# Splits of the fillers' weights ahead of the substitution, four tiles of them for three, and the loop for crowded experts inside group 10: one hybrid block on one core

## The chip, the cores and the metric

The kernel runs on one core of a Trainium2 chip. The time is device microseconds of one execution; the kernel before took 1620.69 us, the median of three runs from 1618.52 to 1622.68.

## The reference, cut to what matters

One residual block on 512 frames of width 1024, with three branches that are gated, projected and summed, and then a mixture of experts:

```
h  = rmsnorm(x); p = h @ w_in                      # conv, RWKV-7 and attention inputs
A  = B * conv3(C * u)                              # short gated convolution
Bw = rwkv7(r, k, v, decay, a)                      # delta-rule state, 8 heads of 64, 512 steps
M  = attention(q, rmsnorm(mem))                    # 4 heads, 256 memory rows
z  = sum_i sigmoid(h @ W_g_i + b_g_i) * (branch_i @ W_p_i)
x  = x + z @ w_o
h2 = rmsnorm(x)
g  = argmax(softmax(h2 @ w_router_group))          # one group of 8 experts
e  = top2(softmax(h2 @ w_router_expert in group g))
x  = x + sum_e weight_e * (silu(h2 @ gate_e) * (h2 @ up_e)) @ down_e
out = rmsnorm(x)
```

All inputs, weights and the output are fp32. There are 64 experts of 1024 x 512, 6 MB each.

## The kernel before, in words

**Dense products.** A weight tile of 128 x 512 arrives in fp32 (`wsrc`) and is split in `split_w` (L77 to L86): ScalarE (ACT) copies it to `wh` (L82, a rounded form), and then `wl` = `wsrc` - `wh` (L85) is made on GpSimd (POOL), or for every third tile on VectorE (DVE). `mm3` (L92) makes of it 12 matmuls of 128 x 512, three for each of four steps of k: `wh` by the high part of the activations, `wh` by the low part, `wl` by the high part. The tiles with the tag "f" have three buffers, those with "r" two.

**Fillers.** RWKV-7 is done in two passes (`rwkv_pass`), each on four heads in chunks of 64. Each pass has one long stretch on DVE: a triangular system is solved by substitution, 31 steps of a product (`tmp`, L405) and a sum (`Xb`, L407), after four transposes into `Ub` (L397) and before two transposes out of `Xb` (L412, L413). The first result of these is `X`, for which the next matmuls of TensorE (PE) wait (L425). Meanwhile PE runs dense products that do not hang on the pass: gates (`gate`, L538), projections (`proj`, whose DVE work is L543 and L545) and the convolution branch (`cu`, `cv`, `ych`, `ycl`, L557 to L569). They are written ahead of the pass or beside it, use the tag "f" and the PSUM name "pf", and are called fillers here. A scheduler puts the instructions of each engine in order when the program is built, by priority: an instruction written earlier has priority over a later one, and what is written under `tc.high_priority(n)` is moved up by n places.

**From the passes to the experts.** After the second pass come the fillers that were not needed as cover, then eight rounds of the last projection (L670 to L675) with a chain `G`, `z`, `zh`, `zl` on DVE and ACT (L543, L545, L673, L674), then eight rounds of `w_o` (L688 to L720), each with a slice `xs` of the input, its square `sq` and a sum `sqs` of the squares on POOL (L708), then the router.

**Experts.** The 64 experts are done in 20 groups of three (g = 0 to 19) and a last group of four. A group has nine loads of 2 MB from SyncE's (SP's) queue, all issued at L640: three `gate` matrices into ring `wa`, three `up` into `wb`, three `down` into `wc`. `select` gathers the group's tokens by matmuls with a one-hot matrix (`oe`, `oT`, `pt`, L820 to L841), `into` multiplies by gate or up (`pc`, `pco`), `hidden` makes the hidden activations `ht`, and `mlp` multiplies by down (`pr`) and adds to `acc` (L883). `mlp` of group g also runs `select` and the gate product of group g + 1, passed as the generator `nxt`. `ahead(3)` issues the next three loads where a ring's last readers have been written; `owed` counts such issues that are to be left out.

An expert with more than 32 tokens is finished by `overflow` (L966 on), a loop whose count is only known on the chip; a pass of it loads one whole expert into ring `wc`. With these inputs it makes no pass. It stands at the start of group 10: `mlp(9)` runs without a next group, the loop follows, then the remaining loads of group 10 are issued, then `begin(10)` selects and multiplies by gate. The SP rows at L969 are the loop's compare and branch.

Of the kernel before, what the change touches and what calls it, by code (L numbers as in the profile page):

```python
# [7 lines left out]
F32 = mybir.dt.float32  # L8
F32R = mybir.dt.float32r
I32 = mybir.dt.int32  # L10
U32 = mybir.dt.uint32
AF = mybir.ActivationFunctionType
OP = mybir.AluOpType
# [4 lines left out]
T, D, MEM = 512, 1024, 256  # L18
NT, ND = T // 128, D // 128
# [23 lines left out]
GE, NG = 3, 20  # L43
# [7 lines left out]
def block_kernel(ctx, tc, I, out):  # L51
    nc = tc.nc
# [11 lines left out]
    def f(ap):  # L64
        return ap.bitcast(F32)
# [5 lines left out]
    wpool = {"f": pro.enter_context(tc.tile_pool(name="wf", bufs=2))}  # L71
# [4 lines left out]

    def split_w(src, shape, tag="f"):  # L77

        n = 3 if tag == "f" else 2
        wh = wpool[tag].tile([128] + shape, F32R, name="wh", bufs=n)  # L80
        wl = wpool[tag].tile([128] + shape, F32R, name="wl", bufs=n)
        nc.scalar.activation(wh, src, AF.Copy)  # L82
        cnt[0] += 1
        eng = nc.gpsimd if cnt[0] % 3 else nc.vector
        eng.tensor_tensor(wl, src, f(wh), op=OP.subtract)  # L85
        return wh, wl  # L86

    def mm3(ps, wh, wl, xh, xl, nk, first=True, last=True, skip=False):
# [31 lines left out]
    yk = keep2.enter_context(tc.tile_pool(name="yk", bufs=1))  # L120
    yr = [yk.tile([128, T], F32, name=f"yr{k}") for k in range(4)]
# [51 lines left out]
    with ExitStack() as attn:  # L173
# [3 lines left out]
        with tc.tile_pool(name="xin", bufs=1) as xin, tc.tile_pool(name="mem", bufs=1) as mp:  # L177
# [3 lines left out]
            xs = xin.tile([128, NT, D], F32, name="xs")  # L181
# [16 lines left out]
            for k in range(ND):  # L198
                wv = wpool["r"].tile([128, 512], F32, name="wv", tag="wsrc", bufs=4)
                nc.sync.dma_start(wv, I["w_v"][k * 128:(k + 1) * 128])  # L200
                wh, wl = split_w(wv, [512], "r")
# [82 lines left out]
    for nm, t in (("ln_x_w", lnw), ("ln_x_b", lnb)):  # L284
        v = I[nm].rearrange("o (q e j c) -> o q e j c", q=2, e=2, j=2)
# [285 lines left out]
    for m in range(ND):  # L571
        g = fil.tile([128, T], F32, name="g", bufs=2)
# [32 lines left out]
    sl, so = (late.tile([128, 2, NT], F32, name=n) for n in ("sl", "so"))  # L605
    vals = late.tile([128, 2, NT, 6], BF, name="vals")
    ring = {n: ctx.enter_context(tc.tile_pool(name="ring" + n, bufs=1, side="right")) for n in "ab"}
# [37 lines left out]
    def ahead(n):  # L645

        for _ in range(n):
            if owed[0]:
                owed[0] -= 1
            else:  # L650
                next(loads, None)
# [31 lines left out]


    tp = pro.enter_context(tc.tile_pool(name="tp", bufs=2))
    sqs = tp.tile([128, T], F32, name="sqs", bufs=1)
    lg = psum.tile([128, NT, 80], F32, name="lg", tag="pc")
    for m in range(ND):  # L688
        xs = yk.tile([128, NT, 128], F32, name="xs", tag=f"yr{(m + 3) % 4}")
        nc.sync.dma_start(xs, I["x"].rearrange("(t p) d -> p t d", p=128)[:, :, m * 128:m * 128 + 128])  # L690
        ps = acc_r("pf")
        for t in range(NT):
            nc.tensor.matmul(ps[:, t * 128:(t + 1) * 128], xs[:, t], ident, is_transpose=True,
                             start=t == 0, stop=False, skip_group_check=True)
        dense(ps, I["w_o"][m], lambda k: zh[k], lambda k: zl[k], first=False)
        ahead(2)
        x2t = tp.tile([128, T], F32, name="x2t")
        nc.scalar.activation(x2t, ps, AF.Copy)
        sq = sqs if m == 0 else tp.tile([128, T], F32, name="sq")
        nc.scalar.activation(sq, ps, AF.Square)  # L700
        if m == 1:
            sr = tp.tile([128, 1], F32, name="sr", bufs=1)
            nc.scalar.activation(sr, sq[:, 0:1], AF.Sqrt)
        for t in range(NT):
            nc.tensor.matmul(lg[:, t, 0:72], x2t[:, t * 128:(t + 1) * 128], wr[:, m], start=m == 0 and t == 0,
                             stop=False, skip_group_check=True)
        if 0 < m < ND - 1:
            nc.gpsimd.tensor_tensor(sqs, sqs, sq, op=OP.add)  # L708
        if m >= ND - 2:
            s = sqs if m == ND - 2 else sq  # L710
            for t in range(NT):
                nc.tensor.matmul(lg[:, t, 72:73], s[:, t * 128:(t + 1) * 128], one, start=False,
                                 stop=m == ND - 1 and t == NT - 1, skip_group_check=True)
        pt = acc_r("pr")
        for t in range(NT):
            nc.tensor.transpose(pt[:, t * 128:(t + 1) * 128], x2t[:, t * 128:(t + 1) * 128], ident)
        nc.scalar.activation(acc[:, :, m * 128:m * 128 + 128], pt.rearrange("p (t c) -> p t c", t=NT), AF.Copy)
        if m < ND - 1:
            keep_x2(m, pt)
# [131 lines left out]
                ahead(GE)  # L851
            yield ps

    def hidden(sel, pg, wu, rows, nxt):

        *_, pu = into("pco", sel, wu, rows)
        next(nxt, None)
        hid = mo.tile([128, 512], F32, name="hid")
        nc.scalar.activation(hid, pg, AF.Silu, scale=sel[2])
        nc.vector.scalar_tensor_tensor(hid, pu, sel[2], hid, op0=OP.mult, op1=OP.mult)  # L860
        ht = mo.tile([128, 4, 128], F32, name="ht")
        ps = psum.tile([128, 4, 128], F32, name="pc")
        for k in range(4):
            pe.transpose(ps[:, k], hid.rearrange("s (p k) -> s k p", k=4)[:, k], ident)
        nc.scalar.activation(ht, ps, AF.Copy)
        next(nxt, None)
        return ht
# [14 lines left out]
                pe.matmul(pm[:, u], oh[:, (t + u) * 128:(t + u + 1) * 128], y, start=i == 0, stop=i == 1)  # L882
        nc.vector.tensor_tensor(acc[:, t:t + n, cs], acc[:, t:t + n, cs], pm, op=OP.add)  # L883

    def mlp(sel, pg, wu, wd, rows, nxt=iter(()), wg=None):

        next(nxt, None)
        ht = hidden(sel, pg, wu, rows, nxt)
        py = [psum.tile([128, 512], F32, name="pr", bufs=2) for n in range(2)]
        for k in range(4):  # L890
            for n in range(2):
                for a, r in enumerate(rows):
                    pe.matmul(py[n][r], ht[:, k, r], wd(a, k * 1024 + n * 512, 512),
                              start=k == 0, stop=k == 3, skip_group_check=True)
        if len(rows) > 1:
            ahead(GE)
        nsel = next(nxt, None)
        gate = into("pc", nsel, wg, rows) if nsel else iter(())
        for n in range(2):
            ys = weighted(py[n], sel)  # L900
            pg = next(gate, None)
            for t in range(NT):
                combine(t, slice(n * 512, n * 512 + 512), ys, sel[3])
                if t % 2:
                    pg = next(gate, None)
        for pg in gate:
            pass
        return nsel, pg
# [57 lines left out]
    def overflow():  # L966

        n_over = nc.values_load(nov[0:1, NO:NO + 1], min_val=0, max_val=NO)
        with tc.For_i(0, n_over, 1):  # L969
            e = nc.values_load(nov[0:1, 0:1], engines=[mybir.EngineType.SP], min_val=0, max_val=63)  # L970
            t = ring["c"].tile([128, 3, 4096], F32, name="wc")
            ws = []
            for i, n in enumerate(("gate", "up", "down")):
                nc.sync.dma_start(t[:, i], whole(I["w_exp_" + n][bass.ds(e, 1)].rearrange("o k c -> (o k) c")))
                ws.append(lambda a, o, c, i=i: t[:, i, o:o + c])
            mlp(*begin(so, 0.0, ws[0], ALL), ws[1], ws[2], ALL)
            V.tensor_scalar(so, so, 128.0, None, op0=OP.subtract)
            sh = mo.tile([128, NO], I32, name="sh")
            V.tensor_copy(sh[:, 0:NO - 1], nov[:, 1:NO])
            V.tensor_copy(nov[:, 0:NO - 1], sh[:, 0:NO - 1])  # L980

    def begin(at, base, wg, rows):
        *_, sel = select(at, base)
        *_, pg = into("pc", sel, wg, rows)
        return sel, pg

    def weights(g):

        if g < NG:
            s = nc.values_load(whose[0:1, g:g + 1], engines=[mybir.EngineType.PE], min_val=0, max_val=GE - 1)  # L990

        def of(n):
            def w(a, o, c):
                if g < NG and a == GE:
                    return B[g, n][:, bass.ds(s, 1), o:o + c].rearrange("p s c -> p (s c)")
                return W[g, n][a][:, o:o + c]
            return w

        return [of(n) for n in ("gate", "up", "down")]

    ALL, EACH = (slice(0, 128),), tuple(slice(a * CAP, a * CAP + CAP) for a in (1, 2, 3, 0))
    sel = select(sl, 0.0, V)
# [53 lines left out]
    V.tensor_scalar(nof[:, 0:NO], nof[:, 0:NO], 63.0, None, op0=OP.min)  # L1056
    V.tensor_copy(nof[:, NO:NO + 1], bs[:, 64:65])
    V.tensor_copy(nov, nof)
    V = nc.vector
    for g in range(NG + 1):  # L1060
        if g == NG // 2:
            overflow()
            ahead(GE)
            w = weights(g)
            now = begin(sl, 128.0 * g, w[0], EACH)
        if g == NG:
            for _ in loads:
                pass
            finish(*now, *w[1:], EACH)
        elif g + 1 == NG // 2:  # L1070
            owed[0] = GE
            mlp(*now, *w[1:], EACH)
        else:
            v = weights(g + 1)
            now = mlp(*now, *w[1:], EACH, select(sl, 128.0 * (g + 1)), v[0])
            w = v


# [91 lines left out]
```

## Time and profile before

| | |
|---|---|
| runs before, median (lowest to highest) | 1620.69 us (1618.52 to 1622.68) |
| the profiled execution's own time | 1627.8 us |
| its span, and instructions | 1626.0 us, 23087 |
| mean granted clock of PE | 0.935 |
| busy: PE, DVE, ACT, POOL | 1445.8, 615.0, 362.4, 236.2 us |
| read from HBM, mean rate | 452.47 MB, 280 GB/s |

The span divides in two. To about 696 us it is the three branches, the merge and the router; from there the experts. In the first part PE does most of the work under a chain that passes to DVE in each pass; in the second the loads are back to back. In the rows below "a <- b" after a wait is what ended it, `out<-in` are the program's tiles, and xN counts instructions. PEclk is the granted clock of PE as a share of full speed.

### The profile page before, as it was taken

The page shows a single profiled execution, that of the slowest core. Times are in us where ns is not written, and L with a number is a line of the kernel's source. Part 1 is how long each engine was busy: PE and PEld are TensorE (multiplying, and loading weights), DVE is VectorE, ACT ScalarE, POOL GpSimd, SP SyncE. Part 2 cuts the span into 40 slices and gives each one's busy share as a digit, 9 for nine tenths or more (in the row PEclk, how much of TensorE's full clock was granted, in tenths as well). Part 3 has the DMA queues.
Part 4 walks back from the last instruction along what each step waited for, and adds up shares of the span by engine and source line. Part 5 has one row for each costly group of instructions (what it writes and reads, how often), then busy time and mean ns, then how long its engine had stood idle before and what let it go on. Part 6 is the DMA issues. An engine that isn't in the chain of part 4 may idle for free.

```text
span 1626.0 us, 23087 instructions
## 1 busy us (share of the span) xinstructions
PE 1445.8 (89%) x9526; PEld 900.1 (55%) x9526; DVE 615.0 (38%) x1137; ACT 362.4 (22%) x688; POOL 236.2 (15%) x200
## 2 busy tenths in 40 slices
PE   7999978999988999699888899878988888998865
PEld 5777757776766778544444445434444444444423
DVE  5342799257692460532222221213222222222212
ACT  6443432534423444110000000000000000000003
POOL 3224342244431333000000000000000000000001
PEclk9999999899996999799999999998999999999977
DMA  7321212021111195389999999998999999999994
GB/s 247 99 83 49 68 52 79 33 72 59 39 58 40 59 321 189 155 362 430 429 430 429 431 430 431 430 430 376 430 429 430 430 430 431 430 430 430 430 416 190
DMA packets 67721, 456.09 MB, mean 280 GB/s; under 512 B 8984, under 2 KB 15008, under 8 KB 44320
## 3 DMA queue, kind: packets, MB, share of 16 engines
q1 hardware_dynamic: 66016, 453.53, 68.2%
q8 instruction: 78, 1.28, 0.3%
q10 hardware_dynamic: 1600, 1.06, 0.2%
q14 instruction: 27, 0.22, 0.0%
HBM read 452.47 MB, written 2.10 MB: 280 GB/s over the span
## 4 chain that ended last, share of the span: by engine, by line
PE 50%; DMA 32%; DVE 13%; issue 2%; SPq 1%; ACT 1%; POOL 0%; DVEq 0%; ACTq 0%; POOLq 0%
DMA wa<-in_w_exp_gate_dram 27%; PE pc L735 11%; PE pf L92 11%; PE pr L92 7%; PE pf L735 6%; PE pt L735 3%; PE pco L735 2%; DMA wb<-in_w_exp_gate_dram 2%; PE pr L735 2%; DMA wb<-in_w_exp_up_dram 2%; DVE tmp L405 2%; DVE Xb L407 1%; DVE Ub L397 1%; DMA wa<-in_w_exp_down_dram 1%; DVE wl L85 1%
## 5 line engine op out<-in xcount | busy, mean ns | idle before, releaser
L735 PE MATMUL pc<-wa,xgt 128*32 128x512 f32 (+1 forms) x1328 | 218.1, 635 | 73.4 <-DMA wa<-in_w_exp_gate_dram 73.4
L883 DVE TENSOR_TENSOR acc<-acc,pf 128x512 f32<-128x512 f32 x168 | 109.4, 684 | 209.2 <-PE pf L735 209.0
L85 POOL TENSOR_TENSOR wl<-wsrc,wh 128x512 fp32r<-128x512 f32 x101 | 139.8, 1388 | 292.5 <-ACT wh L82 246.6
L735 PE MATMUL pt<-oT,x 128*128 128x128 f32 x1344 | 163.7, 282 | 12.0 <-DVE eg L735 7.1
L735 PEld LDWEIGHTS pt<-oT,x 128*128 128x128 f32 x1344 | 158.4, 197 | 28.7 <-issue 23.2
L735 PE MATMUL pco<-wb,xgt 128*32 128x512 f32 (+1 forms) x1312 | 165.4, 600 | 7.3 <-issue 4.2
L735 PE MATMUL pr<-wc,ht 128*32 128x512 f32 (+2 forms) x1312 | 156.3, 595 | 4.6 <-DMA wc<-in_w_exp_down_dram 3.8
L951 POOL TENSOR_TENSOR acc<-acc,x 128x1024 f32<-128x1024 f32 x3 | 7.1, 2357 | 946.9 <-ACT junk L948 946.9
L735 PEld LDWEIGHTS pc<-wa,xgt 128*32 128x32 f32 x1328 | 40.7, 112 | 180.2 <-DMA wa<-in_w_exp_gate_dram 103.2
L82 ACT ACTIVATE wh<-wsrc 128x512 fp32r<-128x512 f32 x152 | 95.7, 630 | 174.7 <-PE pf L92 86.9
L92 PE MATMUL pf<-hh,wl 128*128 128x512 f32 x288 | 122.8, 426 | 9.9 <-DVE wl L85 9.7
L92 PE MATMUL pf<-hh,wh 128*128 128x512 f32 x288 | 121.0, 420 | 5.8 <-DVE Xb L407 4.1
L735 PEld LDWEIGHTS pco<-wb,xgt 128*32 128x32 f32 x1312 | 76.9, 111 | 86.0 <-issue 65.6
L873 ACT ACTIVATE yh<-pr,wr 128x512 fp32r<-128x512 f32 (+1 forms) x44 | 29.4, 668 | 413.9 <-PE pf L735 224.1
L92 PE MATMUL pf<-hl,wh 128*128 128x512 f32 x288 | 119.7, 416 | 0.0
L735 PEld LDWEIGHTS pr<-wc,ht 128*32 128x32 f32 x1312 | 50.4, 111 | 91.6 <-issue 79.6
L860 DVE SCALAR_TENSOR_TENSOR hid<-pco,wr,hid 128x512 f32<-128x512 f32 x21 | 15.8, 751 | 215.2 <-PE pco L735 215.2
L735 PEld LDWEIGHTS pf<-yh,oh 128*128 128x128 f32 x176 | 37.9, 215 | 91.1 <-issue 46.8
L735 PE MATMUL pf<-yh,oh 128*128 128x512 f32 (+1 forms) x176 | 85.9, 490 | 1.3 <-ACT yh L873 1.0
L874 DVE SCALAR_TENSOR_TENSOR yl<-pr,wr,yh 128x512 fp32r<-128x512 f32 (+1 forms) x44 | 31.8, 723 | 140.5 <-ACT yh L873 140.5
L829 DVE TENSOR_TENSOR xgt<-pt,gft 128x512 f32<-128x512 f32 x40 | 27.7, 692 | 129.0 <-PE pt L735 129.0
L735 PE MATMUL pf<-yl,oh 128*128 128x512 f32 (+1 forms) x176 | 75.3, 430 | 1.2 <-DVE yl L874 1.2
(400 smaller groups left out, 2098.9 us busy)
## 6 DMA issues: line engine op xcount, KB each, us to landing
wc<-in_w_exp_down_dram SPq DMA_DIRECT2D x60, 2048.0 KB, 30.3
wa<-in_w_exp_gate_dram SPq DMA_DIRECT2D x60, 2048.0 KB, 24.6
wb<-in_w_exp_up_dram SPq DMA_DIRECT2D x59, 2048.0 KB, 31.2
wsrc<-in_w_in_dram SPq DMA_DIRECT2D x56, 256.0 KB, 2.6
wsrc<-in_w_gate_dram SPq DMA_DIRECT2D x48, 256.0 KB, 2.6
wsrc<-in_w_branch_dram SPq DMA_DIRECT2D x24, 256.0 KB, 2.7
wa<-in_w_exp_gate_dram SPq DMA_DIRECT2D x12, 512.0 KB, 6.0
wb<-in_w_exp_up_dram SPq DMA_DIRECT2D x12, 512.0 KB, 6.8
```

The costliest lines, as they stand in the source:

```text
L82: nc.scalar.activation(wh, src, AF.Copy)
L85: eng.tensor_tensor(wl, src, f(wh), op=OP.subtract)
L92: nc.tensor.matmul(ps, w(k), x(k), start=first and k == 0 and i == 0, stop=last and k == nk - 1 and i == 2, skip_group_check=skip)
L397: nc.vector.transpose(Ub[rows].rearrange("b t s -> b (t s)"), src.unsqueeze(2).to_broadcast([32, 32, 32 // NB, NB]))
L405: nc.vector.tensor_tensor(tv, Ub[:, s + 1:, s:s + 1].to_broadcast([128, n, s + 1]), Xb[:, s:s + 1, 0:s + 1].to_broadcast([128, n, s + 1]), ...
L407: nc.vector.tensor_tensor(Xb[:, s + 1:, 0:s + 1], Xb[:, s + 1:, 0:s + 1], tv, op=OP.add)
L735: return lambda *a, **k: tc.keep_in_program_order(getattr(self.eng, name)(*a, **k))
L829: V.tensor_tensor(xgt[:, k4:k4 + 4], ps, last(gft[:, k4:k4 + 4], 128), op=OP.mult)
L860: nc.vector.scalar_tensor_tensor(hid, pu, sel[2], hid, op0=OP.mult, op1=OP.mult)
L873: nc.scalar.activation(yh, py, AF.Copy, scale=sel[1])
L874: nc.vector.scalar_tensor_tensor(yl, py, sel[1], f(yh), op0=OP.mult, op1=OP.subtract)
L883: nc.vector.tensor_tensor(acc[:, t:t + n, cs], acc[:, t:t + n, cs], pm, op=OP.add)
```

## The change: three edits

1. `split_w` has four buffers instead of three for the tag "f", and the two instructions of such a split stand under `tc.high_priority(4000)`.
2. To make room, `sqs` takes an existing tile (`yr2`), `xs` goes round three tiles instead of four, and `sq` has one buffer instead of two.
3. `mlp(9)` is now an ordinary one that selects group 10 and multiplies by its gate. In group 10 `hidden` runs first, into a pool of its own; then the loop, which now uses ring `wb`; then three issues that were owed and `mlp(10)` with the finished `ht`, which selects group 11.

```diff
     def split_w(src, shape, tag="f"):
 
-        n = 3 if tag == "f" else 2
-        wh = wpool[tag].tile([128] + shape, F32R, name="wh", bufs=n)
-        wl = wpool[tag].tile([128] + shape, F32R, name="wl", bufs=n)
-        nc.scalar.activation(wh, src, AF.Copy)
+        n = 4 if tag == "f" else 2
         cnt[0] += 1
         eng = nc.gpsimd if cnt[0] % 3 else nc.vector
-        eng.tensor_tensor(wl, src, f(wh), op=OP.subtract)
+        with tc.high_priority(4000) if tag == "f" else ExitStack():
+            wh = wpool[tag].tile([128] + shape, F32R, name="wh", bufs=n)
+            wl = wpool[tag].tile([128] + shape, F32R, name="wl", bufs=n)
+            nc.scalar.activation(wh, src, AF.Copy)
+            eng.tensor_tensor(wl, src, f(wh), op=OP.subtract)
         return wh, wl
...
-    sqs = tp.tile([128, T], F32, name="sqs", bufs=1)
+    sqs = yk.tile([128, T], F32, name="sqs", tag="yr2")
...
-        xs = yk.tile([128, NT, 128], F32, name="xs", tag=f"yr{(m + 3) % 4}")
+        xs = yk.tile([128, NT, 128], F32, name="xs", tag=f"yr{(3, 0, 1)[m % 3]}")
...
-        sq = sqs if m == 0 else tp.tile([128, T], F32, name="sq")
+        sq = sqs if m == 0 else tp.tile([128, T], F32, name="sq", bufs=1)
...
-    def mlp(sel, pg, wu, wd, rows, nxt=iter(()), wg=None):
+    def mlp(sel, pg, wu, wd, rows, nxt=iter(()), wg=None, ht=None):
...
-        ht = hidden(sel, pg, wu, rows, nxt)
+        ht = ht or hidden(sel, pg, wu, rows, nxt)
...
-        nsel = next(nxt, None)
+        nsel = None
+        for nsel in nxt:
+            pass
...
-            t = ring["c"].tile([128, 3, 4096], F32, name="wc")
+            t = ring["b"].tile([128, 3, 4096], F32, name="wb")
...
     for g in range(NG + 1):
-        if g == NG // 2:
-            overflow()
-            ahead(GE)
-            w = weights(g)
-            now = begin(sl, 128.0 * g, w[0], EACH)
         if g == NG:
...
-        elif g + 1 == NG // 2:
+            break
+        ht = None
+        if g == NG // 2:
+
             owed[0] = GE
-            mlp(*now, *w[1:], EACH)
-        else:
-            v = weights(g + 1)
-            now = mlp(*now, *w[1:], EACH, select(sl, 128.0 * (g + 1)), v[0])
-            w = v
+            ht = hidden(*now, w[1], EACH, iter(()), late2)
+            overflow()
+            ahead(GE)
+            w = weights(g)
+        v = weights(g + 1)
+        now = mlp(*now, *w[1:], EACH, select(sl, 128.0 * (g + 1)), v[0], ht)
+        w = v
```

The end of the second pass's substitution on DVE, before (L412 and L413 are the transposes out of `Xb`, L543 the product of a projection's filler, L85 the split):

```order
L407 TENSOR_TENSOR Xb<-Xb,tmp 128x31
L412 STREAM_TRANSPOSE X_2676<-Xb 128x1024
L413 STREAM_TRANSPOSE Ub<-Xb 128x1024
L543 SCALAR_TENSOR_TENSOR g<-g,pf 128x512
L85 TENSOR_TENSOR wl<-wsrc,wh 128x512
L469 COPY RH<-pc 128x128
```

and in the change, where every line number after L80 is higher by one:

```order
L408 TENSOR_TENSOR Xb<-Xb,tmp 128x31
L544 SCALAR_TENSOR_TENSOR g<-g,pf 128x512
L86 TENSOR_TENSOR wl<-wsrc,wh 128x512
L413 STREAM_TRANSPOSE X_2676<-Xb 128x1024
L414 STREAM_TRANSPOSE Ub<-Xb 128x1024
L470 COPY RH<-pc 128x128
```

A split and a product of the fillers that stood behind the transposes now stand ahead of the first of them. Along the rest of the substitution each split stands 4 to 13 rows earlier. Counted to the first transpose out of `Xb`, DVE has as many splits as before in both passes (17, and 12 from the first pass's result on); new ahead of it are one `ycl` (L75) in the first pass and this `g` in the second. In the normalisation of the first pass's result (L497 to L510) two splits now stand that stood around it, in the second pass's two instead of one, and in the chain `G`, `z`, `zh`, `zl` three instead of two.

The loads on SP around the loop, before (`nov` holds the loop's count; L974 are the loop's own loads):

```order
L640 DMA wc<-in_w_exp_down_dram 128x4096 x3
L640 DMA wa<-in_w_exp_gate_dram 128x4096 x3
L640 DMA wb<-in_w_exp_up_dram 128x4096
L968 TENSOR_LOAD nov
L969 COMPARE_AND_BRANCH
...
L969 UNCONDITIONAL_BRANCH
L640 DMA wb<-in_w_exp_up_dram 128x4096 x2
L968 ISA x2
L640 DMA wc<-in_w_exp_down_dram 128x4096 x3
```

and in the change:

```order
L641 DMA wa<-in_w_exp_gate_dram 128x4096 x3
L641 DMA wb<-in_w_exp_up_dram 128x4096 x3
L641 DMA wc<-in_w_exp_down_dram 128x4096 x3
L971 TENSOR_LOAD nov
L972 COMPARE_AND_BRANCH
...
L972 UNCONDITIONAL_BRANCH
L641 DMA wa<-in_w_exp_gate_dram 128x4096 x3
L971 ISA x2
L641 DMA wb<-in_w_exp_up_dram 128x4096 x3
```

Before, the loop stands behind the fourth load of group 10; now it stands behind all nine. In both, nothing is issued between the loop's first compare and its last branch but the loop's own loads, and SP's branch into the loop waits for all loads issued so far and for the other four engines.

Of the fillers' matmuls on PE, counted in order, these stand ahead of a place in the program:

| place on PE | before | after |
|---|---|---|
| first matmul of the first pass's low-rank products | 145 | 152 |
| first `AR` by `BK` product of the first pass | 210 | 210 |
| second block's first product of `sk` by `cst` | 228 | 231 |
| last `AR` by `BK` product of the first pass | 279 | 277 |
| `X`, first pass | 444 | 448 |
| first pass's result transposed | 578 | 589 |
| second pass's first product of `sk` by `cst` | 601 | 610 |
| first `AR` by `BK` product of the second pass | 650 | 654 |
| last `AR` by `BK` product of the second pass | 723 | 726 |
| `X`, second pass | 869 | 876 |
| second pass's result transposed | 1002 | 1012 |
| first `w_o` round's router product | 1179 | 1179 |

## Rows read from the trace of the kernel before

**Rows 1.** The page: busy time by engine, and its chain by engine.

```profile
PE 1445.8 (89%) x9526; PEld 900.1 (55%) x9526; DVE 615.0 (38%) x1137; ACT 362.4 (22%) x688; POOL 236.2 (15%) x200
...
PE 50%; DMA 32%; DVE 13%; issue 2%; SPq 1%; ACT 1%; POOL 0%; DVEq 0%; ACTq 0%; POOLq 0%
```

**Rows 2.** Chain that ended last, start of the experts: start us, length us, what.

```profile
688.90 7.00 PE pc L735 x64
...
773.34 28.69 DMA wa<-in_w_exp_gate_dram
```

**Rows 3.** The same chain around the loop.

```profile
1089.26 26.84 DMA wb<-in_w_exp_up_dram
...
1116.41 0.04 DVEq L969
```

**Rows 4.** Windows around the loop: length, busy us of PE, PEld, DVE, ACT, POOL, PEclk, DMA, GB/s.

```profile
1100.00:1110.00 10.00, 8.66 (x57) 3.30 (x49) 3.83 (x6) 1.38 (x2) 0.00 (x0) 1.00 1.01 431
1110.00:1120.00 10.00, 4.93 (x13) 3.12 (x14) 4.98 (x9) 0.00 (x0) 0.00 (x0) 0.68 0.55 208
1120.00:1130.00 10.00, 10.00 (x80) 9.29 (x83) 2.07 (x5) 0.60 (x1) 0.00 (x0) 0.80 1.01 429
```

**Rows 5.** Windows at the end of the first pass's substitution.

```profile
270.00:280.00 10.00, 5.61 (x19) 3.92 (x18) 9.64 (x24) 1.20 (x2) 2.62 (x2) 0.87 0.22 78
280.00:290.00 10.00, 9.29 (x100) 7.34 (x100) 4.30 (x4) 6.24 (x8) 0.00 (x0) 0.79 0.08 28
290.00:300.00 10.00, 10.00 (x83) 7.37 (x80) 0.44 (x2) 4.30 (x9) 3.26 (x6) 0.66 0.09 28
```

**Rows 6.** Windows at the end of the second pass's substitution.

```profile
480.00:490.00 10.00, 5.04 (x20) 3.22 (x18) 9.52 (x18) 1.84 (x3) 4.12 (x3) 0.95 0.09 25
490.00:500.00 10.00, 5.89 (x47) 4.77 (x48) 5.48 (x11) 3.80 (x4) 1.28 (x1) 0.54 0.16 56
500.00:510.00 10.00, 10.00 (x113) 8.05 (x110) 0.69 (x1) 4.70 (x9) 1.01 (x3) 0.64 0.09 28
510.00:520.00 10.00, 10.00 (x55) 7.18 (x53) 1.44 (x5) 3.54 (x9) 3.05 (x6) 0.51 0.07 27
```

**Rows 7.** Timeline of DVE in the first pass's substitution: start us, us, what.

```profile
264.48 0.42 DVE L407 TENSOR_TENSOR Xb<-Xb,tmp 128x252 f32<-128x252 f32 x1
264.93 1.39 DVE L405 TENSOR_TENSOR tmp<-Ub,Xb 128x247 f32<-128x247 f32 x1
...
276.46 0.68 DVE L85 TENSOR_TENSOR wl<-wsrc,wh 128x512 fp32r<-128x512 f32 x1
```

**Rows 8.** Timeline of POOL, both passes: in brackets the idle time before, and its releaser.

```profile
264.52 1.53 POOL L85 TENSOR_TENSOR wl<-wsrc,wh 128x512 fp32r<-128x512 f32 x1 [1.27 <-ACT wh L82]
...
451.18 1.30 POOL L85 TENSOR_TENSOR wl<-wsrc,wh 128x512 fp32r<-128x512 f32 x1 [6.78 <-ACT wh L82]
```

**Rows 9.** Chain that ended last, the transposes into Ub of the second pass.

```profile
449.87 2.04 DVE Ub L397
451.92 2.02 DVE Ub L397
```

**Rows 10.** PE's waits from 0 to 696 us: total us, times, longest us.

```profile
PE pf L92 <- DVE wl L85: 9.7, 3, 3.6
...
PE pr L425 <- DVE X L412: 5.8, 2, 5.1
```

**Rows 11.** Chain that ended last, from the second pass to w_o.

```profile
567.18 15.07 PE pf L92 x66
582.27 0.70 DVE G L543
...
607.26 0.70 DVE zl L674
608.00 0.73 PE pf L92 x2
...
611.31 4.81 PE pf L92 x21
```

More of the change, by code (lines that the diff above doesn't have):

```diff
@@ L852, in into, with hidden @@
             yield ps
-    def hidden(sel, pg, wu, rows, nxt):
+    def hidden(sel, pg, wu, rows, nxt, pool=mo):
         *_, pu = into("pco", sel, wu, rows)
@@ L860, in hidden @@
         nc.vector.scalar_tensor_tensor(hid, pu, sel[2], hid, op0=OP.mult, op1=OP.mult)
-        ht = mo.tile([128, 4, 128], F32, name="ht")
+        ht = pool.tile([128, 4, 128], F32, name="ht")
         ps = psum.tile([128, 4, 128], F32, name="pc")
@@ L1058, in block_kernel @@
     V.tensor_copy(nov, nof)
+    late2 = ctx.enter_context(tc.tile_pool(name="late2", bufs=1))
     V = nc.vector
     for g in range(NG + 1):
-        if g == NG // 2:
-            overflow()
-            ahead(GE)
-            w = weights(g)
-            now = begin(sl, 128.0 * g, w[0], EACH)
         if g == NG:
```

## The prediction

> **What bounds the kernel now.** I read the page first, then the chain of waits, then windows of time where the chain changes hands. On the page [rows 1] PE is busy 1445.8 of 1626.0 us, but the chain that ended last is only half PE; 32% is loads and 13% DVE. So the kernel has stages with different limits.
>
> From the first gate product at 688.90 [rows 2] the experts run behind loads: every group puts one wait for `wa` of some 28 us into the chain (28.69 us at 773.34 is the first). What a full stretch moves is 431 GB/s [rows 4], so a 2 MB load takes 2.097 / 0.431 = 4.87 us, and a group of nine takes 43.8. Here PE is not the bound. Two things follow: whatever moves the start at 688.90 moves the end by as much, and every microsecond in which loads stand still counts in full.
>
> The loads stand still once. Around the loop the window from 1110 to 1120 moves 208 GB/s where its neighbours move 431 and 429 [rows 4]: (430 - 208) / 430 x 10 = 5.2 us lost. The chain says why [rows 3]: a load issued at 1089.26 is waited for to 1116.1, the loop's branch ends at 1116.45, and loads are issued again only then.
>
> Ahead of the experts, the ends of the two substitutions decide. DVE is busy 9.64 of 10 us from 270 to 280 [rows 5] and 9.52 from 480 to 490 [rows 6], PE 5.61 and 5.04: DVE is the bound, PE the cover. When `X` comes, PE goes on, at a lower clock: 0.79 and 0.66 in the two windows after the first pass's `X`, and 0.54, 0.64 and 0.51 from 490 to 520 in the second. A level of 1.2 GHz is half of 2.4, so a window of mean 0.54 has lost 4.6 us of its ten: 2.1 + 3.4 = 5.5 us after the first `X`, 4.6 + 3.6 + 4.9 = 13.1 after the second. PE waits for DVE's splits 9.7 us in three pieces and for `X` 5.8 in two [rows 10].
>
> **The change, part by part.**
>
> *Fillers.* A split feeds 12 matmuls, and 21 of them take 4.81 us [rows 11], 0.229 each. The table in the section on the change shows where they went; I sort its stretches by who leads there. Where PE leads: +7 ahead of the first pass, +3 between its two blocks of low-rank products, +7 between the first `X` and the transposed result, -2 and -1 on the way into the second pass, +3 after the second `X`, -10 in the rest. That is +7 matmuls, +1.6 us. The same 7 leave stretches that DVE leads (-7, -5 and -5 in the pass's preparation, +6 and +4 under the substitutions), where they cost or save PE nothing: PE has idle time there, 4.4 of ten us in the first window [rows 5].
>
> *DVE's chains.* A split on DVE takes 0.68 us [rows 7], and `ycl` and `g` are of the same shape. To `X` there are no more splits than before, so the earlier places cost nothing, but `ycl` in the first pass and `g` in the second now stand ahead of `X`: 2 x 0.68 = +1.4. Two splits in the first normalisation: between 0 and 2 x 0.68, since fillers cover part of it; I take half, +0.7. In the second, 66 matmuls of fillers (15.07 us) stand behind it [rows 11] and hide the split. The chain from `G` at 582.27 to `zl` at 607.96 [rows 11] has no cover left, since PE starts its next matmul on `zl` at 608.00: one split more, +0.7 (a zero is the other end, as each round also waits for PE). Together +2.8, bounds +1.4 to +3.5.
>
> *POOL.* Two thirds of the splits are POOL's, and they are dear to DVE. A `tmp` that stands beside a POOL split takes 1.39 us, its neighbour 0.42 [rows 7, 8]: about 1.0 us each. The transposes into `Ub` took 2.04 and 2.02 with a POOL split (451.18) beside the second [rows 8, 9], so there it is free. A fourth tile lets one more split start ahead in each window: 0 to 2 x 1.0 us, and below zero if the extra one falls under the transposes. Since +6 and +4 matmuls are less than one split, I take 0 and keep +2 as the end. The Trainium skill ("SBUF — State Buffer", section "SBUF: two separate sides") calls this an exclusive lock: of DVE with two SBUF inputs and GpSimd, whichever comes second stands still until the first has finished. By that, priority for POOL's splits speaks against the change, and the sum would have the whole +2; the rows of `tmp` and of the transposes (one input) agree with it.
>
> *Tiles given up.* `xs` and `sq` are needed once in a round of `w_o`, which has at least its 21 matmuls of 4.81 us on PE [rows 11]; the POOL sum that reads `sq` is of a split's shape, 1.30 us [rows 8]. So one buffer is enough while PE leads: cost 0. If that cover goes, six rounds could each wait for a sum, 6 x 1.3 = 8 us; I give that no weight, as 3.5 us would have to go first.
>
> *The loop.* Before, 1 + 3 loads are in flight at the entry and the fourth one runs alone at the end. After, the order on SP puts all nine ahead, and the branch still waits for the last; behind it six loads are free to go at once. So loads run dry all the same, behind `down` of group 10 instead of the first `up`. `down` lands six loads behind gate, 29 us. `up` lands after 14.6, its product takes as long as gate's (7.00 us for 64 matmuls [rows 2]), and the rest of `hidden` is a few matmuls; so PE should be done by 22 to 25 and not come later than the loads. The gap is between none (-5.2) and doubled (+5.2, if the end of `hidden` came late). Three loads end together instead of one alone, so the old gap may get a little shorter; I choose a fifth of it, -1.0.
>
> *Sum:* +1.6 + 2.8 + 0 + 0 - 1.0 = +3.4 us. The profiled execution took 1627.8 us by its own clock (span 1626.0), which is 7.1 above the median of the runs; it would come to 1631.2. Taken to the median, 1620.7 + 3.4 = **1624.1 us**. About 0.3%, or 4.9 us, is what a measurement of this kernel can tell from no change: from 1615.8 to 1625.6 it counts as the same.
>
> **The rivals.**
>
> *A. The waits for the splits were on the path.* If the splits' new places give PE work without a break, the 9.7 us [rows 10] leave the path, not only PE's idle time: 1624.1 - 9.7 = 1614.4; and if the clock in the second pass then loses only what the first loses, another 13.1 - 5.5 = 7.6 less, 1606.8. For it: these are PE's longest waits for a filler. Against: DVE is busy 95% or more under them, and X hangs on DVE. Chance 0.25.
>
> *B. The pause moves against `X` (slower).* In the first pass the last split on DVE, at 276.46 [rows 7], comes late, and PE then has fillers until shortly before `X`; in the second PE has none left in its last 5 us and waits up to 5.1 us for `X` [rows 10]. The clock loses 5.5 us after the first and 13.1 after the second [rows 5, 6]. If every split is early, the first pass too uses its fillers up and pauses in one piece at the end, and then restarts slowly as the second does now: +7.6, 1631.7, and up to 1633.7 with POOL's 2 us. It decides if PE's pause directly ahead of the first `X` becomes like that ahead of the second. For it: the order on DVE has all splits earlier. Against: the number of fillers ahead of `X` grows too. Chance 0.25. The Trainium skill ("TensorE: Matmul & The Clock Gate", section "HAM oscillation — how this bites in real kernels") tells of kernels whose every burst restarts at half rate after a wait. [...]
>
> *C. The gap at the loop goes.* If the loads behind the loop start without a break, -5.2 instead of -1.0: 1619.9. Against: the order on SP still holds every issue back behind the branch. Chance 0.12.
>
> *D. Nothing moves.* The order is only an order: a split still waits for its load, ACT's copy and a free tile, and POOL idles 1.27 to 6.78 us ahead of one, each time until ACT's `wh` [rows 8]. If tiles, not priority, are what lacks, all stays: 1620.7. Chance 0.06.
>
> **How the numbers follow.** My forecast has 0.32, of which 0.08 lies above 1625.6 (DVE's and POOL's terms at their upper ends). Faster: A, 0.25, and 0.02 for C together with a part of A, 0.27. The same: 0.24 + 0.10 + 0.06 + 0.01 of B, 0.41. Slower: 0.24 + 0.08 = 0.32. Both signs hold much, so the forecast's own range is 1618.5 to 1627.8: the low bounds give +1.6 + 1.4 - 5.2 = -2.2, the high ones +1.6 + 3.5 + 2 = +7.1, without a doubled gap. For eight times in ten I take in B wholly, and with it the doubled gap (1633.0), and of A its first value with some room: 1610 to 1634.
>
> **What the changed profile would show.** Right: PE's waits for DVE's `wl` below 4 us; DVE still 95% busy until `X` in both passes; the first gate product some 4 us later; one gap in the loads of about 4 us, some 24 us later than before. For A the pass ends earlier by 5 us or more and the windows behind `X` have a higher clock; for B the windows behind the first `X` fall to about 0.55. The prediction is wrong if the time from the start to the first gate product moves by more than 5 us, or if no window around the loop falls under 400 GB/s.

## The result, and the profile after

The changed kernel takes 1638.1 us, the median of five runs from 1636.71 to 1645.26; the kernel before takes 1620.01 beside it. The ratio is 1.0115, with a 95% interval from 1.0098 to 1.0131: 18 us slower. The forecast was 1624.1 with no measurable change, and the range ended at 1634.

The page after, with busy time and the chain by engine, in the order of [rows 1]:

```profile
PE 1449.8 (89%) x9526; PEld 898.3 (55%) x9526; DVE 622.5 (38%) x1137; ACT 362.0 (22%) x688; POOL 229.0 (14%) x200
...
PE 48%; DMA 32%; DVE 12%; issue 3%; ACT 2%; SPq 1%; POOL 1%; DVEq 0%; ACTq 0%; POOLq 0%
```

The chain at the start of the experts, as [rows 2]:

```profile
700.80 7.00 PE pc L736 x64
...
787.40 26.43 DMA wa<-in_w_exp_gate_dram
```

The first gate product starts at 700.80 where [rows 2] have 688.90. The profiled execution of before was itself some 7 us above its median, and the difference lies ahead of the gate product. A run below, with the loop moved and all else as before, has the order of before up to there and a typical time (span 1619.0); its first gate product starts at 681.54. Against that one the change is 19.3 us late when the experts begin, and 15.9 at the end of the span. So the loss is made in the first part. In the rest of this section the change is compared with that run, called loop_alone, where nothing else is said. Traces of one order differ by some microseconds: room_alone, a run below with the order of before, begins the experts at 685, and splits_alone, with the change's order up to there, at 702. A difference of single stretches is good to no more than that.

PE's waits from 0 to 696 us after the change (total, times, longest), as [rows 10]:

```profile
PE pr L426 <- DVE X L413: 13.0, 2, 8.4
...
PE pf L93 <- DVE z L544: 7.5, 2, 3.8
...
PE pf L93 <- DVE g L544: 6.0, 2, 3.0
```

The 9.7 us for DVE's `wl` in [rows 10] are gone from the list, as the change meant. In their place PE's fillers wait 13.5 us for `z` and `g` (3.4 in loop_alone): these are the products that empty a filler's PSUM tile, and in three of the four waits a split of DVE's stands ahead of them, by up to 6 us. And the wait for `X` grew from 5.8 [rows 10] to 13.0: from 0.88 to 4.59 us at the first and from 5.14 to 8.41 at the second, against loop_alone.

Windows cut at the arrival of each `X` (the end of its transpose), ten microseconds ahead and twenty behind, after the change (291.26 and 509.58); columns as in [rows 4]:

```profile
281.26:291.26 10.00, 5.46 (x16) 4.02 (x16) 9.70 (x23) 1.15 (x2) 1.26 (x1) 0.71 0.18 54
291.26:311.26 20.00, 19.95 (x176) 15.72 (x177) 1.80 (x4) 10.73 (x17) 3.26 (x6) 0.55 0.05 16
...
499.58:509.58 10.00, 1.64 (x8) 1.02 (x6) 9.35 (x24) 0.63 (x1) 2.77 (x3) 0.71 0.23 71
509.58:529.58 20.00, 19.95 (x176) 15.63 (x177) 1.59 (x3) 9.95 (x15) 3.78 (x7) 0.55 0.09 32
```

and the same places in loop_alone:

```profile
270.87:280.87 10.00, 4.79 (x13) 3.15 (x12) 9.74 (x23) 1.85 (x3) 1.27 (x1) 0.83 0.23 79
280.87:300.87 20.00, 19.94 (x188) 15.95 (x188) 3.46 (x8) 11.10 (x19) 3.27 (x6) 0.74 0.08 28
...
481.87:491.87 10.00, 2.18 (x9) 1.16 (x7) 9.38 (x22) 0.63 (x1) 1.85 (x2) 0.77 0.23 79
491.87:511.87 20.00, 19.95 (x187) 15.97 (x187) 3.54 (x7) 10.96 (x19) 4.56 (x7) 0.69 0.05 16
```

Ahead of the first `X` PE does no less work than without the change (5.46 us of ten for 4.79), but its pause lies at the end, as the wait for `X`. Behind it the clock is mostly at the lower of its two levels, a mean of 0.55 instead of 0.74: 9.0 us of clock lost instead of 5.2. Behind the second `X` 9.0 us are lost instead of 6.2; the trace of the kernel before has 0.59 there, 8.2 us, so little of that is clearly the change's.

Windows cut at the first instruction of each stage in both traces give the account up to the select of group 0. Idle is the length less PE's busy time; lost clock is the length times one less the granted clock, and part of it falls into idle time.

| stretch | loop_alone: us, PE idle, lost clock | after: us, PE idle, lost clock |
|---|---|---|
| start to the first low-rank product | 159.1, 13.6, 0 | 162.5, 14.1, 0 |
| to the first `AR` by `BK` product | 22.0, 0.9, 0 | 25.3, 4.3, 1.8 |
| second low-rank block to the first `Ub` | 31.7, 4.0, 1.6 | 32.6, 5.8, 1.6 |
| first `Ub` to `X` | 46.3, 7.9, 3.2 | 49.4, 8.3, 3.5 |
| product with `X` to the normalisation | 55.9, 0, 5.0 | 58.8, 0.2, 8.8 |
| fourth low-rank block to the second `Ub` | 30.5, 2.6, 1.8 | 33.7, 4.5, 3.4 |
| second `Ub` to `X` | 44.4, 10.1, 3.1 | 45.6, 9.6, 5.5 |
| product with `X` to the normalisation | 56.5, 0.1, 6.2 | 58.8, 0.2, 8.8 |
| all to the select of group 0, others included | 672.0, 62.6, 31.0 | 690.7, 72.8, 45.0 |

PE is idle 10.2 us longer, and busy 8.5 us longer (617.95 for 609.46) with as many matmuls; that is the 18.7 us. The 14.0 us of clock lost more lie partly in either. The growth is spread: 3.3 us ahead of the first low-rank product, 3.3 and 3.2 in two preparations of a pass, 3.1 and 1.2 from `Ub` to `X`, 2.9 and 2.3 behind the two `X`.

### The profile page after: what moved, and what is told of

Read it like the earlier page. It is cut to its first block, busy times and chain, and to the rows that moved or that the text cites. A ratio compares the mean times of both kernels' runs of the same rounds, so it can differ in the third digit from the quotient of the medians.

```text
span 1634.9 us, 23077 instructions
## 1 busy us (share of the span) xinstructions
PE 1449.8 (89%) x9526; PEld 898.3 (55%) x9526; DVE 622.5 (38%) x1137; ACT 362.0 (22%) x688; POOL 229.0 (14%) x200
## 4 chain that ended last, share of the span: by engine, by line
PE 48%; DMA 32%; DVE 12%; issue 3%; ACT 2%; SPq 1%; POOL 1%; DVEq 0%; ACTq 0%; POOLq 0%
DMA wa<-in_w_exp_gate_dram 27%; PE pf L93 11%; PE pc L736 11%; PE pr L93 8%; PE pf L736 6%; PE pt L736 2%; DMA wc<-in_w_exp_down_dram 2%; PE pr L736 2%; PE pco L736 2%; DMA wb<-in_w_exp_gate_dram 2%; DVE Xb L408 2%; DVE tmp L406 2%; DMA wa<-in_w_exp_down_dram 1%; SPq L641 1%; DVE wl L86 1%
## 5 line engine op out<-in xcount | busy, mean ns | idle before, releaser
L736 PE MATMUL pc<-wa,xgt 128*32 128x512 f32 (+1 forms) x1328 | 223.3, 641 | 76.3 <-DMA wa<-in_w_exp_gate_dram 71.9
L86 POOL TENSOR_TENSOR wl<-wsrc,wh 128x512 fp32r<-128x512 f32 x101 | 134.3, 1332 | 295.5 <-ACT wh L85 267.8
L85 ACT ACTIVATE wh<-wsrc 128x512 fp32r<-128x512 f32 x152 | 95.5, 629 | 184.1 <-PE pf L93 78.5
L93 PE MATMUL pf<-hh,wl 128*128 128x512 f32 x288 | 119.0, 413 | 0.0
```

The source lines that it names most:

```text
L93: nc.tensor.matmul(ps, w(k), x(k), start=first and k == 0 and i == 0, stop=last and k == nk - 1 and i == 2, skip_group_check=skip)
L736: return lambda *a, **k: tc.keep_in_program_order(getattr(self.eng, name)(*a, **k))
```

## The experiments

Each ratio is to runs of the kernel before on the same chip, with its 95% interval.

**The parts of the change.** *loop_alone*: the loop as in the change, splits and tiles as before.

> Only the move of the loop into group 10; splits as before, three tiles, no priority. Theory 1 (the order of the splits costs nearly all of the +18 us): the two profiles show the loads 5.2 us short around the loop before and about 6.4 us after, so +1 us: 1621, within 1618 to 1624. Theory 2 (the loop in its new place holds up more than its gap, PE coming back cold with group 10 half done): +6 us or more, 1626 or later. Theory 3 (the move helps and hides in the sum): 1616 or earlier. The first gate product stays where it was (688.9 us in the profile of before) under all three.

Measured: 1622.03 us, ratio 1.0008 (0.9999 to 1.0018). The windows around the loop in its new place:

```profile
1120.00:1130.00 10.00, 6.37 (x55) 3.25 (x46) 0.75 (x1) 0.60 (x1) 0.00 (x0) 0.95 0.91 388
1130.00:1140.00 10.00, 4.73 (x28) 1.87 (x32) 2.07 (x4) 0.00 (x0) 0.00 (x0) 0.53 0.53 197
1140.00:1150.00 10.00, 10.00 (x95) 7.13 (x85) 1.44 (x2) 0.69 (x1) 0.00 (x0) 1.00 1.00 424
```

Against 430 GB/s that is 1.0 + 5.4 + 0.1 = 6.5 us, where [rows 4] had 5.2. The gap moved and did not close; theories 2 and 3 are out. The expectation had the first gate product stay at 688.9; it starts at 681.54, with the order unchanged.

*splits_alone* is the change without the loop's move.

> Everything about the splits (priority, four tiles, the tiles given up for them), loop as before. Theory 1: +17 us, 1637, the first gate product at 700 us or later as in the changed kernel (700.8). Theory 2: +12 or less, 1632 or earlier, the rest being the loop's. Theory 3: later than the whole change, 1640 or more.

Measured: 1638.34 us, ratio 1.0111 (1.0095 to 1.0128). The splits are the whole loss. The next three runs take it apart.

```diff
priority_3_tiles, against splits_alone (and without the three edits that make room)
-        n = 4 if tag == "f" else 2
+        n = 3 if tag == "f" else 2
tiles_4, against before (with the three edits that make room)
-        n = 3 if tag == "f" else 2
+        n = 4 if tag == "f" else 2
room_alone, against before: only the three edits to sqs, xs and sq
```

> Priority for the splits with the three tiles of before, loop and other tiles as before. If priority puts splits into DVE's chains and that is the cost, most of it stays: +10 to +17, 1630 to 1637. If the splits can only run ahead with a fourth tile, so that both are needed: within 4 us of before, 1616 to 1624.

Measured: 1634.14 us, ratio 1.0084 (1.0069 to 1.0099).

> Four tiles and the tiles given up for them, no priority, loop as before. If priority is the cost: no slower than before, 1614 to 1622, perhaps faster, since a split has more room to run ahead in DVE's idle time. If the run-ahead itself is the cost (splits beside DVE's chains, whoever orders them): +5 us or more, 1625 or later.

Measured: 1631.56 us, ratio 1.0072 (1.0051 to 1.0094).

> Only the tiles given up (sqs, xs, sq); three tiles for the splits, no priority, loop as before. The order of the instructions is that of before. If four tiles alone cost 12 us by the splits' run-ahead: within 2 us of before, 1617 to 1622. If it was the tiles given up: 1626 or later, the rounds of w_o longer than 7.3 us.

Measured: 1621.66 us, ratio 1.0015 (1.0003 to 1.0026). Priority alone costs 0.84%, the fourth tile 0.57% beyond the tiles given up, which cost 0.15%. Both let splits run ahead, in different orders, and each costs. So it is not priority alone.

**What a POOL split does to DVE.** In the first preparation, the timeline of DVE after the change:

```profile
168.21 2.62 DVE L332 TENSOR_TENSOR_SCAN cw<-one,sa 128x64 f32<-128x64 f32 x8
...
177.73 1.83 DVE L345 SCALAR_TENSOR_TENSOR sk<-rk,pv,sk 128x512 f32<-128x512 f32 x1
```

and of POOL beside it:

```profile
168.91 1.40 POOL L86 TENSOR_TENSOR wl<-wsrc,wh 128x512 fp32r<-128x512 f32 x1 [1.29 <-ACT wh L85]
...
177.75 1.26 POOL L86 TENSOR_TENSOR wl<-wsrc,wh 128x512 fp32r<-128x512 f32 x1 [3.65 <-ACT wh L85]
```

The same rows of DVE in loop_alone, and POOL's split of that time:

```profile
164.76 1.57 DVE L331 TENSOR_TENSOR_SCAN cw<-one,sa 128x64 f32<-128x64 f32 x8
168.90 3.34 DVE L342 RECIPROCAL sk<-sk 128x512 f32<-128x512 f32 x1
...
173.09 0.75 DVE L344 SCALAR_TENSOR_TENSOR sk<-rk,pv,sk 128x512 f32<-128x512 f32 x1
```

```profile
169.98 2.53 POOL L85 TENSOR_TENSOR wl<-wsrc,wh 128x512 fp32r<-128x512 f32 x2
```

Before, the two splits ran beside the reciprocal, which still takes 3.34 us with them. After, splits stand beside the scan and beside `sk`, and each holds DVE up by 1.05 to 1.08 us. The windows over the stretch show what that does to PE, first loop_alone and then the change:

```profile
159.00:181.00 22.00, 21.15 (x113) 15.55 (x112) 17.27 (x28) 12.80 (x19) 13.08 (x9) 1.00 0.21 61
```

```profile
162.00:188.00 26.00, 21.71 (x111) 15.57 (x111) 21.83 (x28) 12.56 (x19) 14.49 (x10) 0.93 0.20 61
```

DVE's 28 instructions take 21.83 us instead of 17.27. Only 2.1 of these 4.6 us are the scan and `sk`. Most of the rest is a `BK` and an `AR` product beside POOL's own `BK` product: 1.75 and 1.70 us for 0.68 and 0.69, where in loop_alone POOL's pair was the longer one (4.75 us for 4.03). In the trace of the kernel before, with the order of loop_alone, the same two take 1.76 and 1.62; there the stretch is 22.9 us long, DVE takes 19.25 and PE is idle 1.9. So the splits' new places are worth some 2 us of DVE here. The stretch is 21.9 to 22.9 us long in the three traces with the order of before, and 25.3 and, in splits_alone, 24.2 with that of the change. In loop_alone fillers carried PE over the stretch (idle 0.9 us); in the change DVE is longer and the fillers, used up earlier, are fewer, and PE stands 4.3 us.

To test it, POOL's part of a split was replaced by something that reads nothing.

```diff
-        eng.tensor_tensor(wl, src, f(wh), op=OP.subtract)
+        if eng is nc.gpsimd:
+            nc.gpsimd.memset(f(wl), 0.0)
+        else:
+            eng.tensor_tensor(wl, src, f(wh), op=OP.subtract)
```

> The kernel before, but POOL's share of the splits (two of three) is replaced by a fill with zeros of the same tile: the correction term of those tiles is left out. POOL then reads nothing while DVE works. Theory P (a POOL split that reads beside DVE stops DVE about 1.0 us, and this is what the change multiplies): earlier than before, by 4 us or more where such stops lie on the path today, 1616 or earlier. Theory C (cover: fillers are used up where PE leads and are missing where DVE leads): within 3 us of before.

Measured: 1597.28 us, ratio 0.9864 (0.9847 to 0.988).

> The change of the splits (priority and four tiles, loop as before) with the same fill in place of POOL's share. Theory P: the cost against the kernel before with the fill falls from 18 us to 6 or less. Theory C: it stays at 12 or more, since the order on PE is nearly the same. In between: both.

Measured: 1605.0 us, ratio 0.9905 (0.9888 to 0.9922). The groups of the substitution's steps by line, from 0 to 700 us, in the kernel before (busy us, mean ns, idle before):

```profile
L405 DVE TENSOR_TENSOR tmp<-Ub,Xb 128x31 f32<-128x31 f32 (+15 forms) x62 | 31.0, 500 | 1.7
L407 DVE TENSOR_TENSOR Xb<-Xb,tmp 128x31 f32<-128x31 f32 (+15 forms) x62 | 27.1, 437 | 1.7
```

and with the fill (line numbers three higher):

```profile
L408 DVE TENSOR_TENSOR tmp<-Ub,Xb 128x31 f32<-128x31 f32 (+15 forms) x62 | 23.2, 374 | 1.7
L410 DVE TENSOR_TENSOR Xb<-Xb,tmp 128x31 f32<-128x31 f32 (+15 forms) x62 | 22.2, 358 | 1.7
```

The steps of both passes take 45.4 us instead of 58.1. And the cost of the splits' new order falls from 1.11% to 0.9905 - 0.9864 = 0.41%, some 7 us. That is a little more than theory P allowed and less than theory C asked, so both have a part; by this pair about 11 of the 18 us hang on POOL's splits. The order of the fillers is kept: 144, 211, 444 and 869 of their matmuls stand ahead of the first low-rank product, the first `AR` by `BK` product and the two `X` in before_pool_fill (145, 210, 444 and 869 in the kernel before), and 152, 210, 448 and 876 in splits_pool_fill, as in the change. The first preparation takes 22.5 us in the one and 22.3 in the other: without POOL's splits its loss is gone. Of the 9.0 us that splits_pool_fill is behind at the gate product (667.7 for 658.7), 7.0 are there at the first low-rank product (158.6 for 151.6). The fill is shorter than the split (a mean of 526 ns for 1388) and does not wait for ACT's `wh`, so the 11 us hold POOL's own time too; no run has a fill of the split's length.

**Splits on DVE.** Every filler's `wl` on DVE, first with the change's order, then with that of before:

```diff
-        eng = nc.gpsimd if cnt[0] % 3 else nc.vector
+        eng = nc.gpsimd if cnt[0] % 3 and tag != "f" else nc.vector
```

> The change of the splits, loop as before, but every filler's wl is made on DVE (0.68 us each) and none on POOL. Theory P: a split on DVE costs DVE's chains less than one on POOL that stops it 1.0 us; DVE gets 2/3 of some 100 splits more, but only those in the chains count: faster than the change, 1625 to 1635. Theory C alone: DVE's chains get longer by 0.68 us for each split in them, some 25 more, so 1645 or later.

Measured: 1622.48 us, ratio 1.0024 (1.0011 to 1.0036). A little better than theory P's range, and far from theory C's.

> The kernel before (three tiles, no priority, loop as before) with every filler's wl on DVE. Theory P: POOL's splits stop DVE 6 to 7 us in each substitution (the steps took 27.9 us with them and 21.1 without), a split on DVE takes 0.68 us instead of about 1.0, and 28 and 20 more matmuls of fillers stand ahead of the two X: faster than before, 1605 to 1615. Theory C (DVE's chains are the bound, and every split in them counts): 1625 or later.

Measured: 1612.55 us, ratio 0.9947 (0.993 to 0.9964). This version is faster than the kernel before by 0.53% (9 us) and than the change by 1.7%. Its DVE and POOL groups of splits to 700 us, and the windows at the first `X`:

```profile
L85 DVE TENSOR_TENSOR wl<-wsrc,wh 128x512 fp32r<-128x512 f32 x125 | 93.1, 750 | 87.9 <-ACT wh L82 77.1 <-PE pf L693 8.1 <-PE pf L92 2.4
L85 POOL TENSOR_TENSOR wl<-wsrc,wh 128x512 fp32r<-128x512 f32 x27 | 35.5, 1315 | 104.4 <-ACT wh L82 104.3
```

```profile
270.00:280.00 10.00, 8.95 (x45) 7.12 (x45) 9.59 (x25) 3.02 (x5) 0.00 (x0) 1.00 0.39 132
280.00:290.00 10.00, 10.00 (x108) 7.75 (x106) 4.64 (x8) 6.78 (x8) 0.00 (x0) 0.76 0.16 53
```

DVE does 74 splits more and the substitution is as long as it was, but PE works more ahead of `X`: 9.00 us of the ten up to its arrival (269.6 to 279.6), where it works 4.95 in the kernel before (272.0 to 282.0). Against this run splits_on_dve, which adds the change's order, is 0.77% slower (1.0024 to 0.9947), some 12 us: with no filler's split on POOL two thirds of the change's 1.11% stay. There each split takes DVE itself 0.75 us, and the order is another (472 and 926 of the fillers' matmuls stand ahead of the two `X` here, 479 and 940 in splits_on_dve), so this pair does not isolate the stops either. Taken together the two pairs put POOL's part at 0.34 to 0.70%, 5 to 11 us.

> Four tiles and the tiles given up for them, no priority, loop as before, every filler's wl on DVE. With POOL's splits the fourth tile cost 12 us. Theory P: without them it costs nothing, within 4 us of before_on_dve's 1612.6: 1608 to 1617. If the run-ahead itself costs (fillers used up early, whoever splits): 1620 or later.

Measured: 1616.85 us, ratio 0.9981 (0.997 to 0.9991). Inside the range in microseconds; by the ratios it is 0.34% above before_on_dve, 5.5 us, which is over the four that theory P allowed. With POOL's splits the fourth tile and its room cost 0.72%. So about half of it goes with POOL's splits, and about half stays whoever splits.

> The kernel before with two of three filler splits on DVE and one on POOL. Theory P: between before and all on DVE, 1612 to 1620. If the gain comes from the order of the fillers rather than from the stops: no gain, 1619 or later, since 13 matmuls fewer than before stand ahead of both X.

```diff
-        eng = nc.gpsimd if cnt[0] % 3 else nc.vector
+        eng = nc.gpsimd if cnt[0] % 3 == 1 or (cnt[0] % 3 and tag != "f") else nc.vector
```

Measured: 1632.49 us, ratio 1.0062 (1.0041 to 1.0083). Theory P missed this: one third of the splits on POOL is slower than two thirds. The other expectation held, no gain where fewer fillers stand ahead of the two `X`. It has 431 and 856 of the fillers' matmuls ahead of the two `X`, the kernel before 444 and 869. So the order that the scheduler makes of the fillers seems to weigh as much as the stops, and the engine of a split changes that order too; no run varies the fillers' order alone.

**The start.** Priority only from the 15th filler split on:

```diff
-        with tc.high_priority(4000) if tag == "f" else ExitStack():
+        fcnt[0] += tag == "f"
+        with tc.high_priority(4000) if tag == "f" and fcnt[0] > 14 else ExitStack():
```

> The change of the splits (four tiles, priority), loop as before, but priority only from the 15th filler split on: the first 159 us are in the order of before, the passes in the order of the change. Theory E (of the change's 18 us some 3 to 6 come from fillers' splits that stand ahead of attention's weights at the start): 1632 to 1635. Theory P alone: 1637 or later.

Measured: 1634.59 us, ratio 1.0073 (1.0051 to 1.0096). In medians 3.8 us better than splits_alone, as theory E said, and by the ratios 0.38%; but the two intervals touch, so a gain is likely and its size open. Its first low-rank product starts at 159.6 us in the profile (before 159.1, the change 162.5, splits_alone 165.2), and the preparation behind it is as long as the change's, 25.0 us.

## Why the prediction was wrong

- **What bounds the kernel: right.** The stages are as described: everything made in the first part shows at 700.80, and the loads behind it keep their pace.
- **POOL: the term that was mis-sized.** "Since +6 and +4 matmuls are less than one split, I take 0 and keep +2 as the end." The price of a stop, 1.0 us, was read rightly [rows 7, 8]; the places were not. I looked for new stops only under the substitutions and counted filler matmuls there. The steps of the substitutions did not change (58.8 us after, 58.1 before). The new stops stand in the preparation of the passes, where the splits moved from beside the reciprocal to beside operations that they stop: 2.1 us for the scan and `sk` of the first pass, in a stretch that grew by 3.3. The runs with the fill put some 11 us on POOL's splits, those with DVE's splits 5. The Trainium skill ("SBUF — State Buffer", section "SBUF: two separate sides") says that a DVE operation with two inputs in SBUF and a GpSimd operation that reads SBUF exclude each other for the whole of an instruction. These rows agree (1.05 us more for the scan and 1.08 for `sk`, nothing for the reciprocal, steps of 374 and 358 ns beside fills that read nothing). By that rule the question to ask of a changed order is which DVE instruction stands beside each POOL one, and I asked it only where the profile already showed a collision.
- **Fillers: the step that failed with it.** "The same 7 leave stretches that DVE leads [...], where they cost or save PE nothing". They were the cover there. The row of the table with -7 is the stretch in which PE's idle time goes from 0.9 to 4.3 us (1.9 in the trace of the kernel before). My assumption that DVE led this stretch already was wrong: in loop_alone PE is busy 21.15 of 22 us in it. But it took the stops too: between the two fill runs the same fillers leave (67 matmuls become 58), and the stretch does not grow.
- **DVE's chains: sign right.** The first `X` does come later by `ycl` and its like (the stretch from `Ub` grew by 3.1 us against the 0.7 I gave it), the second by 1.2 for 0.7. The chain `G` to `zl` showed no loss: from the second normalisation to `G` the change is 1.2 us shorter, and the stretch behind it 0.2 longer.
- **Rival B happened, in part.** The pause moved against the first `X` (a last wait of 4.59 us for 0.88) and the clock behind it fell to the lower level: 3.8 us more lost in the twenty behind it. Behind the second it is 2.8 us more than in loop_alone and 0.8 more than in the kernel before. I gave 7.6, as 13.1 - 5.5; but the 13.1 took three windows for the second `X` against two, and the first of the three holds some 4 us ahead of its arrival. In the twenty microseconds behind each arrival the kernel before lost 5.2 and 8.2, a difference of 3.0. The chance was 0.25, and the rival came on top of the POOL stops, not alone. That the pause's place was the cause is read from the windows; no run varied it by itself.
- **Rival A fell.** The 9.7 us for `wl` did vanish, and 13.5 us for `g` and `z`, 3.4 in loop_alone, took their place: DVE was the bound, so what goes first there makes something else late.
- **The loop: mechanism right.** One gap, behind the group's last `down`, of 6.5 us instead of 5.2; forecast -1.0, measured +1.3 with an interval that reaches zero.
- **The tiles given up** were taken as 0 and cost 0.15%, just clear of nothing.

What stays open: how much of the 18 us is POOL's (5 to 11), and how the rest divides between fillers used up early and the start. The start counts in each pair of traces: the first low-rank product is 3.3 us late in the change, 6.2 in splits_on_dve against before_on_dve and 7.0 in splits_pool_fill against before_pool_fill. The fillers' matmuls that stand there now are part of it, 1.6 us at my price for seven.

## What to carry to other kernels

When work for two engines is moved ahead, list for every stretch what now stands beside what on the engines that exclude each other, above all where the trace shows no collision yet: a harmless neighbour (a reciprocal, a transpose) may have been the reason. Count fillers as cover at every place where the count falls, and ask who takes over when they are gone. Where the bound engine is the one that serves a wait, priority only renames the wait.

## What was not expected of the hardware

- In the kernel before, the steps of the two substitutions are 13 us shorter with the fill than with POOL's splits (45.4 against 58.1 us), and the whole kernel is 22 us shorter (1597.28 against 1619.35), though POOL is busy 15% of the span.
- Of DVE's operations beside a POOL split, the eight-part scan (1.57 to 2.62 us) and the `sk` product (0.75 to 1.83) were held up; the reciprocal of 128 x 512 was not (3.34 us).
- Moving a slow engine's work onto the engine that is the bound was a gain: 74 more splits on DVE, at 0.75 us each, made the kernel 0.53% faster.
